# One 64-column product per head and chunk in an RWKV-7 recurrence, with the value map and the state map stacked

## The chip, the cores and the metric

The kernel runs on one core of a Trainium2 chip. TensorE (PE) multiplies, and its weight loads are listed apart as PEld; VectorE (DVE), ScalarE (ACT) and GpSimd (POOL) do elementwise work, and SyncE (SP) issues the DMAs, in order. The metric is the device time of the whole program in microseconds. The kernel before takes 2608.76 us, the median of 3 runs (2606.76 to 2610.3).

## The reference

A hybrid decoder block: RMSNorm, one input projection whose columns go to two token mixers side by side (an S5 state-space mixer and RWKV-7 time mixing), one output projection with a residual, then a squared-ReLU MLP. 2048 tokens, model width 1024, float32. The change lies in the RWKV-7 recurrence: 8 heads of 64, a 64x64 state per head, decayed and updated once per token.

```python
def step(state, inp):
    r_t, d_t, k_t, v_t, kk_t, a_t = inp
    sa = jnp.einsum('bhvk,bhk->bhv', state, -kk_t)
    state = (state * d_t[:, :, None, :]
             + sa[..., None] * (kk_t * a_t)[:, :, None, :]
             + v_t[..., None] * k_t[:, :, None, :])
    return state, jnp.einsum('bhvk,bhk->bhv', state, r_t)
...
_, ys = lax.scan(step, s0, xs)
```

## The kernel before

The program goes through input stages, the recurrence (`rwkv_phase`), the output projection and the MLP; a planner overlaps neighbouring stages. The recurrence takes 64 tokens at a time: 32 chunks, four to a block of 256 tokens, 8 blocks. The 8 heads stand in 4 pairs (`NP`), so that a pair fills 128 partitions: rows 0–63 are its first head, 64–127 its second.

For a chunk, the output and the next state are linear in the chunk's values and in the state before it. `solve` builds the two maps, `chain` applies them:

- `values` (one unit per pair and block) loads k and v of a pair into one zero-padded tile `bk` (each head on its own diagonal block), and q into `qi`. It forms `ps_k` (L853), masks it into `kT` (DVE L857, ACT L858), and transposes v on PE (`ps_v`, L851) into `vT` (ACT L855). Once per block, q is also loaded as `qS` (L840).
- `units` does the same for the other operands: `ps_b` (L817) into `bQ`, `ps_a` (L826) into `aR`. Each unit's last loads and the strips `abd` (L832) feed `invert`.
- `invert` solves the triangular 16-step systems of a block on DVE (`prod`, `Z`, L876/877), with DMAs in and out (`M`, `zd`, `dtc`, `lo`); `join` finishes the inverse with 32x32 products (`ps_x` L898, `ps_u` L905).
- `solve` (per chunk): POOL spreads the inverse (`DT`, L913), PE multiplies (`ps_pq`, L920), ACT copies into a block-diagonal tile `pq` in two halves (L923, L924), and PE forms `ps_f` (L928) and `ps_h` (L930), four 128x128 products each. DVE adds q and the identity to `ps_f`, which gives `gf`, the map from the state (L934, L935), and `kT` to `ps_h`, which gives `hj`, the map from the values (L936).
- `chain` (per chunk, in two halves of two pairs): per pair `ps_s` = `hj`·`vT` (L949) plus `gf`·`S` (L951), both 128 columns, accumulated in one PSUM bank. Rows 64–127 are the next state, scaled by `em` on DVE into the block-diagonal `S` (L957), rows 0–63 the output, copied by ACT (L958) and stored (L963).

The order on PE is written by hand: the loop over chunks n takes, in turn, the first half of `chain`, a pending `ps_v`, the second half, `ps_pq` of chunk n+2, `ps_b` of a unit 13 ahead, `ps_k` of a value unit 5 ahead, `ps_f` and `ps_h` of chunk n+2, and `ps_a`. Units end at chunk 19 and value units at chunk 27. The other engines and SP are ordered by the scheduler. Value loads wait until the tile they overwrite is free: `bk` and `qi` exist twice (`NB`). Every fp32 matmul runs as two passes on PE, each with its own weight load.

Of the kernel before, what the change touches and what calls it, by code (L numbers as in the profile page):

```python
# [15 lines left out]
P = 128  # L16
# [740 lines left out]
def rwkv_phase(K, f_dram, e_dram, n_dram, y_dram, ntok=2048):  # L757
# [7 lines left out]
    with ExitStack() as st:  # L765
# [11 lines left out]
        S = None  # L777
# [20 lines left out]
        mask = lambda t, n: bc(t.rearrange("p (o x) -> p o x", o=1), [P, n, t.shape[1]])  # L798
# [35 lines left out]
        def values(b, B, p):  # L834

            if p == 0:
                kv = kvs[b % 2]
                for n, shape in (("kT", [P, NCH, NP, P]), ("vT", [P, NCH, NP, P]), ("qS", [P, NP, TB])):
                    B[n] = kv.tile(shape, F32, tag=n, name=n)
                nc.sync.dma_start(out=B["qS"], in_=f_dram[:, :, b, RW["q"]].rearrange("t p n -> p t n"))  # L840
            kT, vT = B["kT"], B["vT"]
            i = (b * NP + p) % NB
            bk, qi = bks[i], qis[i]
            load_pair(bk, b, p, RW["k"])
            nc.sync.dma_start(out=qi[:, 0].rearrange("p c x -> p (c x)"), in_=f_dram[p, :, b, RW["q"]])
            for n in range(2):
                ps = pk("ps_" + "kv"[n])
                for u in range(NCH):
                    o = ps[:, u * P:(u + 1) * P]
                    if n:  # L850
                        pe.transpose(out=o, in_=bk[:, n, u], identity=K.ident)  # L851
                    else:
                        pe.matmul(o, bk[:, n, u], qi[:, :, u], start=True, stop=True)  # L853
                if n:
                    act.copy(out=vT[:, :, p], in_=r4(ps))  # L855
                else:
                    B["last"] = v.tensor_tensor(out=kT[:, :, p, 0:64], in0=r4(ps)[:, :, 0:64], in1=mask(c["mk"], NCH), op=ALU.mult)  # L857
                    act.copy(out=kT[:, :, p, 64:128], in_=r4(ps)[:, :, 64:128])  # L858
                    yield
# [48 lines left out]
        def solve(B, u):  # L908

            aR, kT, bQ, qS, dtc, cpl = B["aR"], B["kT"], B["bQ"], B["qS"], B["dtc"], B["cpl"]  # L910
# [10 lines left out]
            pq = pqs[u % 2]  # L921
            psr = ps.rearrange("p (a q x) -> p a q x", a=NP, q=2)
            act.copy(out=pq[0:64, :, :, 0:64], in_=psr[0:64])  # L923
            act.copy(out=pq[64:128, :, :, 64:128], in_=psr[64:128])  # L924
            yield
            psf, psh = pb("ps_f"), pb("ps_h")
            for p in range(NP):
                pe.matmul(psf[:, p * P:(p + 1) * P], pq[:, p, 1], bQ[:, u, p, 64:192], start=True, stop=True)  # L928
            for p in range(NP):
                pe.matmul(psh[:, p * P:(p + 1) * P], pq[:, p, 0], bQ[:, u, p, 64:192], start=True, stop=True)  # L930
            gf = bt.tile([P, NP, 2, 64], F32, tag="gf", bufs=3, name="gf")
            hj = bt.tile([P, NP, P], F32, tag="hj", bufs=3, name="hj")
            pf = psf.rearrange("p (a q x) -> p a q x", a=NP, q=2)
            v.tensor_tensor(out=gf[:, :, 0], in0=pf[:, :, 0], in1=qS[:, :, u * 64:(u + 1) * 64], op=ALU.add)  # L934
            v.tensor_tensor(out=gf[:, :, 1], in0=pf[:, :, 1], in1=bc(ist, [P, NP, 64]), op=ALU.add)  # L935
            B["last"] = v.tensor_tensor(out=f2(hj), in0=psh, in1=f2(kT[:, u]), op=ALU.add)  # L936
            yield gf, hj

        def chain(b, B, u, gf, hj):
            nonlocal S  # L940
            vT = B["vT"]
            yS = Ys[u % 2 * 64:u % 2 * 64 + 64]
            new = Ss[u % 2]

            for p0 in range(0, NP, 2):
                pss = pc("ps_s")
                for p in range(p0, p0 + 2):
                    o = slice((p - p0) * P, (p - p0 + 1) * P)
                    pe.matmul(pss[:, o], hj[:, p], vT[:, u, p], start=True, stop=S is None)  # L949
                    if S is not None:  # L950
                        pe.matmul(pss[:, o], gf[:, p].rearrange("p q x -> p (q x)"), S[:, p], start=False, stop=True)  # L951

                pv = pss[:, 0:2 * P].rearrange("p (a h x) -> p a h x", a=2, h=2)
                for h in range(2):
                    hs = slice(h * 64, h * 64 + 64)
                    e = em[64:128, p0:p0 + 2, h, b * NCH + u:b * NCH + u + 1]
                    v.tensor_tensor(out=new[hs, p0:p0 + 2, hs], in0=pv[64:128, :, h], in1=bc(e, [64, 2, 64]), op=ALU.mult)  # L957
# [3 lines left out]
            S = new  # L961
# [18 lines left out]
        bks, qis = [T([P, 2, NCH, P], f"bk{i}", vp) for i in range(NB)], [T([P, 2, NCH, 64], f"qi{i}", vp) for i in range(NB)]  # L980
# [4 lines left out]
        pqs = [bt.tile([P, NP, 2, P], F32, tag=f"pq{i}", bufs=1, name=f"pq{i}") for i in range(2)]  # L985
        Ss = [bt.tile([P, NP, P], F32, tag=f"S{i}", bufs=1, name=f"S{i}") for i in range(2)]
        Ys = bt.tile([P, 512], F32, tag="Y", bufs=1, name="Y")
        for t in pqs + Ss:
            g.memset(t, 0.0)
# [4 lines left out]
        for h in range(2):  # L994
            nc.sync.dma_start(out=em[64:128, :, h], in_=e_dram[:, h * 64:h * 64 + 64].rearrange("t p n -> p t n"))
# [743 lines left out]
```

## Time and profile before

| | |
|---|---|
| time, median of 3 runs | 2608.76 us |
| the profiled execution | 2615.8 us, its span 2614.0 us, granted clock 0.974 |
| PE, PEld, DVE, ACT, POOL busy | 2447.6, 2026.7, 1844.5, 1301.2, 851.4 us |
| recurrence, first and last `ps_s` | 694.2 and 981.8 us |
| PE busy in 700–740, 900–940 us | 38.49, 34.53 of 40 us |
| share of 16 DMA engines in 700–740 | 0.71 |

Times are microseconds unless marked ns. In a timeline row stand the start, the length, the engine, the line and the instruction, what is written and read, shapes and count, then in brackets the idle time of the engine before it and what ended that. A row of a group has count, busy time and mean ns of one, and idle time before. `L949` is line 949 of the kernel. Matmuls are pipelined, so one lasts longer than the distance to the next; the cost of a series is read from start to start.

### The profile page before, as it was taken

How to read it: one execution, taken by the hardware profiler on the slowest of the kernel's cores; microseconds unless marked ns; L12 is line 12 of the kernel's file. 1: busy time of each engine (PE TensorE's matmuls, PEld its weight loads, DVE VectorE, ACT ScalarE, POOL GpSimd, SP SyncE). 2: the span in 40 equal slices, each digit the busy share in tenths (PEclk: the TensorE clock that was granted, in tenths of full speed). 3: DMA queues.
4: the chain of work that ended last, by engine and by line, in shares of the span. 5: the costliest groups of instructions: out<-in, count | busy, mean ns of one | idle time of the engine just before them, and what ended most of it. 6: DMA issues, size and time to landing. Idle time of an engine off the chain costs nothing.

```text
span 2614.0 us, 38287 instructions
## 1 busy us (share of the span) xinstructions
PE 2447.6 (94%) x13084; PEld 2026.7 (78%) x13084; DVE 1844.5 (71%) x3194; ACT 1301.2 (50%) x2551; POOL 851.4 (33%) x784
## 2 busy tenths in 40 slices
PE   7999988998889888999899999999969999999997
PEld 7887656786889887888688888888857877777775
DVE  7568897479678768666867669776665556655665
ACT  6355536455444446454566667666543323333333
POOL 1058798601222224121123221332102223322323
PEclk9999989999899998999999999999999999999998
DMA  9656748897776644443475666655585545444544
GB/s 290 210 162 177 215 125 235 245 247 186 176 165 154 136 140 163 143 148 127 170 268 204 212 212 212 229 206 202 188 318 177 178 157 169 166 157 154 184 153 161
DMA packets 542131, 491.50 MB, mean 188 GB/s; under 512 B 187280, under 2 KB 444304, under 8 KB 541936
## 3 DMA queue, kind: packets, MB, share of 16 engines
q1 hardware_dynamic: 541648, 488.00, 60.0%
q8 instruction: 104, 1.70, 0.3%
q10 hardware_dynamic: 288, 1.05, 0.1%
q14 instruction: 91, 0.75, 0.1%
HBM read 303.23 MB, written 180.49 MB: 185 GB/s over the span
## 4 chain that ended last, share of the span: by engine, by line
PE 65%; DVE 13%; DMA 12%; issue 3%; ACT 3%; POOL 2%; SPq 2%; POOLq 0%; DVEq 0%; ACTq 0%
PE ps_ua L1328 13%; PE ps_da L1328 9%; PE ps_ux L1328 7%; PE ps_dx L1328 4%; PE ps_ub L1328 3%; PE ps_db L1328 2%; DMA wraw<-in_w_down 2%; PE ps_o L433 2%; PE ps_o L434 2%; PE ps_o L435 2%; PE ps_z L433 1%; PE ps_z L434 1%; PE ps_z L435 1%; DMA wr<-in_w_in 1%; DVE wl L609 1%
## 5 line engine op out<-in xcount | busy, mean ns | idle before, releaser
L1618 POOL TENSOR_TENSOR acc<-acc,c 128x512 f32<-128x512 f32 x128 | 191.1, 1513 | 500.7 <-ACT c L1622 446.6
L1622 ACT COPY c<-ps_da 128x512 f32<-128x512 f32 x192 | 106.3, 588 | 267.9 <-PE ps_da L1328 266.6
L433 PE MATMUL ps_z<-xh,wh 128*128 128x512 f32 x448 | 183.7, 410 | 16.3 <-DVE zr L617 7.5
L1618 DVE TENSOR_TENSOR acc<-acc,ps_dx 128x512 f32<-128x512 f32 x128 | 87.6, 685 | 133.0 <-PE ps_dx L1328 130.3
L435 PE MATMUL ps_z<-xh,wl 128*128 128x512 f32 x448 | 181.2, 405 | 0.0
L434 PE MATMUL ps_z<-xl,wh 128*128 128x512 f32 x448 | 180.8, 404 | 0.0
L374 ACT CAST hh<-hr 128x512 fp32r<-128x512 f32 x96 | 59.6, 621 | 131.7 <-PE ps_da L1328 92.6
L1425 DVE TENSOR_TENSOR wl<-wraw,wh 128x512 fp32r<-128x512 f32 x124 | 103.8, 838 | 29.5 <-ACT wh L1424 29.2
L433 PEld LDWEIGHTS ps_z<-xh,wh 128*128 128x128 f32 x448 | 86.8, 194 | 41.3 <-DVE zr L617 9.3
L609 DVE TENSOR_TENSOR wl<-wr,wh 128x1024 fp32r<-128x1024 f32 x56 | 86.7, 1548 | 36.8 <-ACT wh L608 35.0
L913 POOL TENSOR_TENSOR DT<-dtc,cst 128x128 f32<-128x128 f32 x128 | 56.0, 468 | 156.9 <-PE ps_pq L920 105.4
L1291 POOL TENSOR_TENSOR ws<-wraw 128x512 f32<-128x512 f32 x28 | 41.2, 1471 | 202.1 <-DMA hs_d<-hh 72.8
L433 PE MATMUL ps_o<-woh,ys 128*128 128x512 f32 x256 | 103.3, 404 | 2.5 <-DVE xrow L1225 2.5
L1424 ACT CAST wh<-wraw 128x512 fp32r<-128x512 f32 x124 | 76.1, 616 | 54.0 <-PE ps_ua L1328 34.9
L434 PE MATMUL ps_o<-wol,ys 128*128 128x512 f32 x256 | 102.5, 401 | 0.2 <-DVE wol L1125 0.2
L435 PEld LDWEIGHTS ps_z<-xh,wl 128*128 128x128 f32 x448 | 86.9, 194 | 19.0 <-issue 0.2
L434 PEld LDWEIGHTS ps_z<-xl,wh 128*128 128x128 f32 x448 | 86.8, 194 | 18.6 <-issue 0.9
L435 PE MATMUL ps_o<-woh,ys 128*128 128x512 f32 x256 | 101.2, 399 | 0.0
L1300 POOL TENSOR_TENSOR ws<-wraw,ws 128x512 f32<-128x512 f32 x28 | 41.7, 1488 | 176.9 <-DVE wl L1425 173.6
L1425 DVE TENSOR_TENSOR wl<-ws,wh 128x512 fp32r<-128x512 f32 x93 | 66.8, 721 | 29.5 <-ACT wh L1424 25.0
L1474 DVE TENSOR_TENSOR hh<-hs,hh 128x512 fp32r<-128x512 f32 x96 | 79.7, 830 | 10.5 <-ACT hh L1473 9.7
L1473 ACT CAST hh<-hs 128x512 fp32r<-128x512 f32 x96 | 59.6, 621 | 53.9 <-DVE hs L1490 21.0
(690 smaller groups left out, 8216.6 us busy)
## 6 DMA issues: line engine op xcount, KB each, us to landing
hs_d<-hh SPq DMA_DIRECT2D x256, 256.0 KB
hs<-hs_d SPq DMA_DIRECT2D x128, 512.0 KB
wraw<-in_w_up SPq DMA_DIRECT2D x62, 512.0 KB
wr<-in_w_in SPq DMA_DIRECT2D x56, 512.0 KB
hr_d<-c SPq DMA_DIRECT2D x96, 256.0 KB
hr<-hr_d SPq DMA_DIRECT2D x96, 256.0 KB
xrow<-in_x SPq DMA_DIRECT2D x32, 512.0 KB
wraw<-in_w_down SPq DMA_DIRECT2D x16, 1024.0 KB
```

Of the source, the lines that this page charges most:

```text
L374: nc.scalar.copy(out=hi, in_=raw)
L433: K.nc.tensor.matmul(out, lh, rh, start=i == 0, stop=False)
L434: K.nc.tensor.matmul(out, lh, rl, start=False, stop=False)
L435: K.nc.tensor.matmul(out, ll, rh, start=False, stop=i == n - 1)
L609: v.tensor_tensor(out=wl, in0=wr, in1=wh.bitcast(F32), op=ALU.subtract)
L1328: K.nc.tensor.matmul(ps, a[k], b[k], start=start and k + i == 0, stop=k == n - 1 and i == 2, skip_group_check=True)
L1424: act.copy(out=hi, in_=o)
L1425: v.tensor_tensor(out=lo, in0=o, in1=hi.bitcast(F32), op=ALU.subtract)
L1473: act.copy(out=hi, in_=o)
L1474: v.tensor_tensor(out=lo, in0=o, in1=hi.bitcast(F32), op=ALU.subtract)
L1618: add = lambda eng, o, s: eng.tensor_tensor(out=o, in0=o, in1=s, op=ALU.add)
L1622: act.copy(out=t, in_=ps)
```

## The change

The two maps of one head are put on top of each other in one 128x128 tile `gh`: rows 0–63 act on the chunk's values, rows 64–127 on the state. The operand is stacked in the same way: `SV` holds, per chunk, the transposed values in rows 0–63 and the state in rows 64–127. So `chain` runs one product of 64 columns per head and chunk, where a pair had two of 128 columns. To get there:

- `KQ` takes the place of `kT`, `qS` and the identity: per head, masked `ps_k` above, q and the identity below. q is loaded into it by two DMAs per value unit; the identity is copied once, by 16 DVE instructions at the recurrence's start.
- v gets a dense tile `vc` of its own, and `bk` holds k alone.
- `pq` is no longer block-diagonal: one ACT copy of 128 partitions. `ps_f` and `ps_h` become one `ps_h`, eight products with 64 rows each, by turns from the first head's rows and the second's, into two banks; two DVE additions of `KQ` give `gh`.
- the state is written into the next chunk's place in `SV`, two DVE instructions per chunk in place of four. The clearing of `pq` and `S` on POOL goes; half of `SV`'s first chunk is cleared.

PE's instructions over one chunk, before (`pq0`, `aq1` and so on are buffers of the tiles above):

```order
L817 MATMUL ps_b_8356<-aq1_5202,ba1_5200 128x192 x2
L853 MATMUL ps_k_8366<-qi1_6803,bk1_6801 128x128 x4
L928 MATMUL ps_f_8373<-bQ_6910,pq0_6811 128x128 x4
L930 MATMUL ps_h_8374<-bQ_6910,pq0_6811 128x128 x4
L826 MATMUL ps_a_8388<-aq1_5202,ba1_5200 128x128 x4
L949 MATMUL ps_s_8400<-vT_7680,hj_8223 128x128
L951 MATMUL ps_s_8400<-S0_6813,gf_8222 128x128
...
L851 MATMUL ps_v_8408<-cst_60,bk1_6801 128x128 x4
L949 MATMUL ps_s_8414<-vT_7680,hj_8223 128x128
L951 MATMUL ps_s_8414<-S0_6813,gf_8222 128x128
...
L920 MATMUL ps_pq_8430<-aR_6909,DT_8423 128x128 x4
```

and with the change:

```order
L816 MATMUL ps_b_9424<-aq1_5202,ba1_5200 128x192 x2
L848 MATMUL ps_k_9437<-qi1_6826,bk1_6822 128x128 x4
L927 MATMUL ps_h_9446<-bQ_7649,pq_9411 128x128
L927 MATMUL ps_h_9447<-bQ_7649,pq_9411 128x128
...
L825 MATMUL ps_a_9459<-aq1_5202,ba1_5200 128x128 x4
L943 MATMUL ps_s_9471<-SV0_6802,gh_9294 128x64 x4
L856 MATMUL ps_v_9478<-cst_60,vc1_6824 64x128 x4
L943 MATMUL ps_s_9484<-SV0_6802,gh_9294 128x64 x4
L918 MATMUL ps_pq_9499<-aR_7648,DT_9492 128x128 x4
```

The order of the steps stays. The two rows of `ps_h` stand for four such pairs in a row, and each row of `ps_s` now covers half a chunk (before, the two rows L949 and L951 stood twice per half).

DVE's queue at the recurrence's start (`L617`, `L377` and `L715` are the last of the input stage, `up` opens the first `join`; `Z` and `prod` are the inversion of the second block). Before, this stretch holds no copy but the two of `qi`; with the change:

```order
L974 COPY KQ1_6801<-cst_60 64x4x64 x4
L617 SCALAR_TENSOR_TENSOR zv_6722<-ps_z_6693,omu_1853,sh_6718 128x512
...
L377 TENSOR_TENSOR sql_6766<-zr_6687,sqh_6765 128x512
...
L715 TENSOR_TENSOR zr_6687<-ps_bv_6764,zv_6722 128x512
L886 STREAM_TRANSPOSE up_6846<-dtc_5394 128x512
...
L974 COPY KQ0_6800<-cst_60 64x4x64 x5
L979 COPY qi0_6825<-cst_60 128x256
```

Eight copies into `KQ1` stand ahead of `zv` and `sql`, eight into `KQ0` between `up` and `qi`.

SP's queue of loads about a block's boundary, before:

```order
L832 DMA abd_7615<-bQ_7614 32x16x32 x4
L804 DMA ba1_5200<-f_d_68 64x8x64 x2
L880 DMA zd_7138<-Z_7718 64x16x32 x2
L865 DMA M_8234<-abd_7615 64x32x32 x2
...
L882 DMA dtc_7787<-zd_7138 128x1x512
L813 DMA aq1_5202<-f_d_68 128x256
L804 DMA bk1_6801<-f_d_68 64x8x64 x2
L891 DMA lo_8396<-zd_7138 32x512 x2
```

and with the change:

```order
L843 DMA KQ0_6800<-f_d_68 64x4x64
L842 DMA bk1_6822<-f_d_68 64x4x64
L831 DMA abd_7166<-bQ_7165 32x16x32 x4
L803 DMA ba1_5200<-f_d_68 64x8x64 x2
L863 DMA M_7747<-abd_7166 64x32x32 x2
L878 DMA zd_6927<-Z_7237 64x16x32 x2
...
L812 DMA aq1_5202<-f_d_68 128x256
L842 DMA bk1_6822<-f_d_68 64x4x64
L844 DMA qi1_6826<-f_d_68 128x256
L845 DMA vc1_6824<-f_d_68 128x256
...
L880 DMA dtc_7306<-zd_6927 128x1x512
L889 DMA lo_7910<-zd_6927 32x512 x2
```

The loads of the value units stand ahead of `dtc` now, and those into `KQ` in a bunch before the strips `abd`.

The diff, without unchanged neighbours:

```diff
-        S = None
...
-        mask = lambda t, n: bc(t.rearrange("p (o x) -> p o x", o=1), [P, n, t.shape[1]])
+        mask = lambda t, n, rows=P: bc(t.rearrange("p (o x) -> p o x", o=1), [rows, n, t.shape[1]])
...
         def values(b, B, p):
-            if p == 0:
-                kv = kvs[b % 2]
-                for n, shape in (("kT", [P, NCH, NP, P]), ("vT", [P, NCH, NP, P]), ("qS", [P, NP, TB])):
-                    B[n] = kv.tile(shape, F32, tag=n, name=n)
-                nc.sync.dma_start(out=B["qS"], in_=f_dram[:, :, b, RW["q"]].rearrange("t p n -> p t n"))
-            kT, vT = B["kT"], B["vT"]
+            KQ, SV = KQs[b % 2], SVs[b % 2]
+            B["KQ"], B["SV"] = KQ, SV
             i = (b * NP + p) % NB
-            bk, qi = bks[i], qis[i]
-            load_pair(bk, b, p, RW["k"])
+            bk, vc, qi = bks[i], vcs[i], qis[i]
+            for h in range(2):
+                hp = slice(h * 64, h * 64 + 64)
+                nc.sync.dma_start(out=bk[hp, :, hp], in_=f_dram[p, hp, b, RW["k"]].rearrange("p (c x) -> p c x", x=64))
+                nc.sync.dma_start(out=KQ[64:128, :, h, p, 0:64], in_=f_dram[p, hp, b, RW["q"]].rearrange("p (c x) -> p c x", x=64))
             nc.sync.dma_start(out=qi[:, 0].rearrange("p c x -> p (c x)"), in_=f_dram[p, :, b, RW["q"]])
-            for n in range(2):
-                ps = pk("ps_" + "kv"[n])
-                for u in range(NCH):
-                    o = ps[:, u * P:(u + 1) * P]
-                    if n:
-                        pe.transpose(out=o, in_=bk[:, n, u], identity=K.ident)
-                    else:
-                        pe.matmul(o, bk[:, n, u], qi[:, :, u], start=True, stop=True)
-                if n:
-                    act.copy(out=vT[:, :, p], in_=r4(ps))
-                else:
-                    B["last"] = v.tensor_tensor(out=kT[:, :, p, 0:64], in0=r4(ps)[:, :, 0:64], in1=mask(c["mk"], NCH), op=ALU.mult)
-                    act.copy(out=kT[:, :, p, 64:128], in_=r4(ps)[:, :, 64:128])
-                    yield
+            nc.sync.dma_start(out=vc.rearrange("p c x -> p (c x)"), in_=f_dram[p, :, b, RW["v"]])
+            ps = pk("ps_k")
+            for u in range(NCH):
+                pe.matmul(ps[:, u * P:(u + 1) * P], bk[:, u], qi[:, :, u], start=True, stop=True)
+            for h in range(2):
+                hp = slice(h * 64, h * 64 + 64)
+                B["last"] = v.tensor_tensor(out=KQ[0:64, :, h, p, 0:64], in0=r4(ps)[hp, :, 0:64], in1=mask(c["mk"][hp], NCH, 64), op=ALU.mult)
+                act.copy(out=KQ[0:64, :, h, p, 64:128], in_=r4(ps)[hp, :, 64:128])
+            yield
+            ps = pk("ps_v")
+            for u in range(NCH):
+                pe.transpose(out=ps[0:64, u * P:(u + 1) * P], in_=vc[:, u], identity=K.ident)
+            act.copy(out=SV[0:64, :, p], in_=r4(ps)[0:64])
...
-            aR, kT, bQ, qS, dtc, cpl = B["aR"], B["kT"], B["bQ"], B["qS"], B["dtc"], B["cpl"]
+            aR, bQ, dtc, cpl = B["aR"], B["bQ"], B["dtc"], B["cpl"]
...
                 pe.matmul(ps[:, p * P:(p + 1) * P], m2(DT, p), aR[:, u, p], start=True, stop=True)
-            pq = pqs[u % 2]
-            psr = ps.rearrange("p (a q x) -> p a q x", a=NP, q=2)
-            act.copy(out=pq[0:64, :, :, 0:64], in_=psr[0:64])
-            act.copy(out=pq[64:128, :, :, 64:128], in_=psr[64:128])
+            pq = bt.tile([P, NP, P], F32, tag="pq", name="pq")
+            act.copy(out=f2(pq), in_=ps)
             yield
-            psf, psh = pb("ps_f"), pb("ps_h")
+            ph = [pb("ps_h") for _ in range(2)]
             for p in range(NP):
-                pe.matmul(psf[:, p * P:(p + 1) * P], pq[:, p, 1], bQ[:, u, p, 64:192], start=True, stop=True)
-            for p in range(NP):
-                pe.matmul(psh[:, p * P:(p + 1) * P], pq[:, p, 0], bQ[:, u, p, 64:192], start=True, stop=True)
-            gf = bt.tile([P, NP, 2, 64], F32, tag="gf", bufs=3, name="gf")
-            hj = bt.tile([P, NP, P], F32, tag="hj", bufs=3, name="hj")
-            pf = psf.rearrange("p (a q x) -> p a q x", a=NP, q=2)
-            v.tensor_tensor(out=gf[:, :, 0], in0=pf[:, :, 0], in1=qS[:, :, u * 64:(u + 1) * 64], op=ALU.add)
-            v.tensor_tensor(out=gf[:, :, 1], in0=pf[:, :, 1], in1=bc(ist, [P, NP, 64]), op=ALU.add)
-            B["last"] = v.tensor_tensor(out=f2(hj), in0=psh, in1=f2(kT[:, u]), op=ALU.add)
-            yield gf, hj
-        def chain(b, B, u, gf, hj):
-            nonlocal S
-            vT = B["vT"]
+                for h in range(2):
+                    hs = slice(h * 64, h * 64 + 64)
+                    pe.matmul(ph[h][:, p * P:(p + 1) * P], pq[hs, p], bQ[hs, u, p, 64:192], start=True, stop=True)
+            gh = bt.tile([P, 2, NP, P], F32, tag="gh", bufs=3, name="gh")
+            for h in range(2):
+                B["last"] = v.tensor_tensor(out=f2(gh[:, h]), in0=ph[h], in1=f2(B["KQ"][:, u, h]), op=ALU.add)
+            yield gh,
+        def chain(b, B, u, gh):
+            SV = B["SV"]
+            n = b * NCH + u
             yS = Ys[u % 2 * 64:u % 2 * 64 + 64]
-            new = Ss[u % 2]
             for p0 in range(0, NP, 2):
                 pss = pc("ps_s")
                 for p in range(p0, p0 + 2):
-                    o = slice((p - p0) * P, (p - p0 + 1) * P)
-                    pe.matmul(pss[:, o], hj[:, p], vT[:, u, p], start=True, stop=S is None)
-                    if S is not None:
-                        pe.matmul(pss[:, o], gf[:, p].rearrange("p q x -> p (q x)"), S[:, p], start=False, stop=True)
-                pv = pss[:, 0:2 * P].rearrange("p (a h x) -> p a h x", a=2, h=2)
-                for h in range(2):
-                    hs = slice(h * 64, h * 64 + 64)
-                    e = em[64:128, p0:p0 + 2, h, b * NCH + u:b * NCH + u + 1]
-                    v.tensor_tensor(out=new[hs, p0:p0 + 2, hs], in0=pv[64:128, :, h], in1=bc(e, [64, 2, 64]), op=ALU.mult)
+                    for h in range(2):
+                        o = (2 * (p - p0) + h) * 64
+                        pe.matmul(pss[:, o:o + 64], gh[:, h, p], SV[:, u, p, h * 64:h * 64 + 64], start=True, stop=True)
+                if n + 1 < nb * NCH:
+                    to = SVs[(n + 1) // NCH % 2][64:128, (n + 1) % NCH, p0:p0 + 2].rearrange("p a (h x) -> p (a h) x", h=2)
+                    v.tensor_tensor(out=to, in0=pss[64:128, 0:2 * P].rearrange("p (a x) -> p a x", a=4),
+                                    in1=bc(em[64:128, 2 * p0:2 * p0 + 4, n:n + 1], [64, 4, 64]), op=ALU.mult)
                 act.copy(out=yS[:, p0 * P:(p0 + 2) * P], in_=pss[0:64, 0:2 * P])
                 if p0 == 0:
                     yield
-            S = new
...
         vp = pool(name="rwv", bufs=1)
-        bks, qis = [T([P, 2, NCH, P], f"bk{i}", vp) for i in range(NB)], [T([P, 2, NCH, 64], f"qi{i}", vp) for i in range(NB)]
+        KQs, SVs = ([T([P, NCH, *d], f"{n}{i}", kvs[i]) for i in range(2)] for n, d in (("KQ", [2, NP, P]), ("SV", [NP, P])))
+        for t in KQs:
+            for h in range(2):
+                for u in range(NCH):
+                    v.tensor_copy(t[64:128, u, h, :, 64:128], bc(ist[64:128], [64, NP, 64]))
+        g.memset(SVs[0][64:128, 0], 0.0)
+        bks, vcs, qis = ([T([P, *d], f"{n}{i}", vp) for i in range(NB)] for n, d in (("bk", [NCH, P]), ("vc", [NCH, 64]), ("qi", [2, NCH, 64])))
         for i in range(NB):
             g.memset(bks[i], 0.0)
             v.tensor_copy(qis[i][:, 1], bc(ist, [P, NCH, 64]))
         bt = pool(name="rwbt", bufs=2, side="right")
-        pqs = [bt.tile([P, NP, 2, P], F32, tag=f"pq{i}", bufs=1, name=f"pq{i}") for i in range(2)]
-        Ss = [bt.tile([P, NP, P], F32, tag=f"S{i}", bufs=1, name=f"S{i}") for i in range(2)]
         Ys = bt.tile([P, 512], F32, tag="Y", bufs=1, name="Y")
-        for t in pqs + Ss:
-            g.memset(t, 0.0)
         psum = {n: pool(name="rwps" + n, bufs=k, space=PSUM) for n, k in (("b", 2), ("c", 2))}
         pb, pc = (lambda name, q=psum[n]: q.tile([P, 512], F32, tag="ps", name=name) for n in "bc")
-        em = bt.tile([P, NP, 2, ntok // 64], F32, tag="em", bufs=1, name="em")
+        em = bt.tile([P, 2 * NP, ntok // 64], F32, tag="em", bufs=1, name="em")
         for h in range(2):
-            nc.sync.dma_start(out=em[64:128, :, h], in_=e_dram[:, h * 64:h * 64 + 64].rearrange("t p n -> p t n"))
+            nc.sync.dma_start(out=em[64:128, h::2], in_=e_dram[:, h * 64:h * 64 + 64].rearrange("t p n -> p t n"))
...
```

## The prediction

> **What bounds the kernel now.** I read the windows of busy time first, to find the recurrence and what is short in it, then the groups of instructions by line, then the timeline of the matmuls, and the waits last. A window row gives start and end, the length, then busy us and the number of instructions of PE, PEld, DVE, ACT and POOL, the granted clock, the share of the DMA engines and GB/s:
>
> ```profile
> 640.00:665.00 25.00, 18.09 (x167) 14.35 (x167) 23.16 (x60) 9.78 (x21) 12.43 (x20) 0.73 0.52 155
> 700.00:740.00 40.00, 38.49 (x412) 37.53 (x413) 35.38 (x129) 20.58 (x53) 8.46 (x23) 1.00 0.71 161
> 900.00:940.00 40.00, 34.53 (x389) 33.29 (x388) 31.79 (x104) 16.02 (x34) 9.76 (x24) 1.00 0.49 116
> 940.00:985.00 45.00, 40.15 (x427) 37.99 (x426) 27.59 (x65) 25.53 (x50) 11.52 (x27) 1.00 0.57 170
> 985.00:1030.00 45.00, 37.55 (x203) 31.51 (x203) 40.28 (x78) 31.16 (x66) 22.83 (x13) 0.85 0.58 193
> ```
>
> Up to 665 us VectorE (DVE) is full. From 700 to 985 TensorE (PE) is, with DVE 4 to 18 us behind it in each window. The recurrence's 32 chunks run there, so work taken from PE counts in full only up to DVE's distance. After 985 DVE leads again, in the output projection, which the change does not edit.
>
> One chunk without the inverse's products, PE alone (start, length, line, product, passes):
>
> ```profile
> 763.93 0.49 PE L949 MATMUL ps_s<-vT,hj 128*128 128x128 f32 x2
> 766.26 1.06 PE L920 MATMUL ps_pq<-aR,DT 128*128 128x128 f32 x8
> 767.15 1.47 PE L817 MATMUL ps_b<-aq,ba 128*128 128x192 f32 x8
> 768.45 1.05 PE L853 MATMUL ps_k<-qi,bk 128*128 128x128 f32 x8
> 769.34 1.06 PE L928 MATMUL ps_f<-bQ,pq 128*128 128x128 f32 x8
> 770.24 1.06 PE L930 MATMUL ps_h<-bQ,pq 128*128 128x128 f32 x8
> 772.02 0.39 PE L949 MATMUL ps_s<-vT,hj 128*128 128x128 f32 x2
> ```
>
> A chunk is 772.02 − 763.93 = 8.09 us with no gap. Each fp32 matmul is two passes, x8 is four matmuls. Eight passes of 128 columns take 769.34 − 768.45 = 0.89 us, 111 ns each; eight of 192 take 768.45 − 767.15 = 1.30 us, 163 ns each. The four pairs of ps_s matmuls are 16 passes, 1.78 us a chunk; ps_f and ps_h together are 16 too, again 1.78.
>
> **The narrower products.** The change runs eight ps_s matmuls of 64 columns where eight of 128 stood: the same 16 passes and 16 weight loads of 128x128, half the columns. What such a pass costs hangs on whether columns or the weight load sets the 111 ns. From 128 to 192 columns a pass grew by 52 ns, 0.81 ns a column; by that line a pass of 64 would be 59 ns. But the trace has short passes with full-width weights:
>
> ```profile
> 29.45 0.29 PEld L131 LDWEIGHTS ps_lam<-cst,lam 32*128 32x128 f32 x2
> 29.46 0.40 PE L131 MATMUL ps_lam<-cst,lam 32*128 32x32 f32 x2
> L131 PEld LDWEIGHTS ps_lam<-cst,lam x4: 181/182/184, 29.5 to 31.3; 32*128 32x128 f32 x4
> L131 PE MATMUL ps_lam<-cst,lam x4: 271/282/292, 29.5 to 31.3; 32*128 32x32 f32 x4
> ```
>
> Two loads of 128 columns end after 0.29 us and one lasts 0.182, so the second starts 0.108 behind the first, though only 32 columns stream; the two matmuls start 0.40 − 0.282 = 0.12 us apart. So I price a 64-column pass at 108 to 120 ns, against 111: between −0.05 and +0.14 us a chunk. I take 0. The low bound is the column line, 16 × (59 − 111) ns = −0.83 us.
>
> The Trainium skill ("TensorE: Matmul & The Clock Gate", section "LDWEIGHTS (loading the stationary operand)") says that a weight load takes as many ns as it has columns, divided by 1.2, whatever its rows: 107 here. The 108 ns agrees, and by it ps_s stays at 1.7 us. Its section "Back-to-back issue gap" lets an isolated matmul of up to 64 columns go in about 60 cycles; that would be the column line's outcome, weighed as a rival below.
>
> **ps_f and ps_h become one ps_h by heads.** Eight matmuls of 128 rows become eight of 64 rows, alternating between rows 0–63 and 64–127, into two banks. If the halves run one after the other nothing is gained: 1.78 us stays. If side by side, 8 × 111 ns = 0.89 us. The trace shows two row groups at work where one head's products meet the next's (32-row tiles):
>
> ```profile
> 655.39 3.24 PE L898 MATMUL ps_x<-up,bQ 32*32 32x32 f32 x61 [1.49 <-DVE up L888]
> 658.41 0.26 PE L905 MATMUL ps_u<-lo,up 32*32 32x32 f32 x1
> 658.45 0.24 PE L898 MATMUL ps_x<-up,bQ 32*32 32x32 f32 x1
> 658.48 0.24 PE L905 MATMUL ps_u<-lo,up 32*32 32x32 f32 x1
> 658.51 0.24 PE L898 MATMUL ps_x<-up,bQ 32*32 32x32 f32 x1
> ```
>
> Inside the first row 61 passes start over 658.41 − 655.39 = 3.02 us, 50 ns apart. Where ps_u of the first head starts while ps_x of the second still has passes, the two lines alternate every 0.03 us: each stream keeps nearly its own pace. So I take 0.89, −0.89 us a chunk.
>
> The Trainium skill ("TensorEngine Tiling (Array Packing)", section "Key Properties") says tiles load and multiply in parallel, and that changing the tiling mode drains TensorE. The second half speaks against this change, and the trace prices it:
>
> ```profile
> 162.95 0.48 PE L669 MATMUL ps_w<-stk,low0h 128*128 128x512 f32 x1
> 163.36 0.50 PE L670 MATMUL ps_w<-stk,lowl 64*128 64x512 f32 x1
> 163.79 0.50 PE L433 MATMUL ps_z<-xh,wh 128*128 128x512 f32 x1
> 164.13 0.39 PE L434 MATMUL ps_z<-xl,wh 128*128 128x512 f32 x1
> 164.35 0.39 PE L435 MATMUL ps_z<-xh,wl 128*128 128x512 f32 x1
> 788.80 1.06 PE L920 MATMUL ps_pq<-aR,DT 128*128 128x128 f32 x8
> 789.79 2.11 PE L898 MATMUL ps_x<-up,bQ 32*32 32x32 f32 x64
> ```
>
> Into 64 rows the step is 0.41 us, out of it 0.43, the next 0.34, where 0.22 is the pace: 0.19 + 0.21 + 0.12 = 0.52 at most. Into ps_x it is 789.79 − 788.80 − 0.89 = 0.10 us alone. A chunk has one more such round trip, ps_k to ps_h to ps_a; between 0.3 and 0.52 I take 0.41. So PE has −0.89 + 0.41 = −0.48 us a chunk.
>
> **DVE and ACT.** These groups change (line, shapes, count, busy us, mean ns, idle before); under them one row of the waits of 892 to 942, and two of the chain of waits:
>
> ```profile
> L957 DVE TENSOR_TENSOR S<-ps_s,em 64x128 f32<-64x128 f32 x127 | 37.3, 294 | 11.7 <-PE ps_s L951 9.0
> L936 DVE TENSOR_TENSOR hj<-ps_h,kT 128x512 f32<-128x512 f32 x32 | 22.0, 687 | 2.0 <-PE ps_h L930 0.7
> L924 ACT COPY pq<-ps_pq 64x512 f32<-64x512 f32 x32 | 18.6, 580 | 0.8
> L934 DVE TENSOR_TENSOR gf<-ps_f,qS 128x256 f32<-128x256 f32 x32 | 13.5, 421 | 9.7 <-PE ps_f L928 9.5
> PE ps_f L928 <- ACT pq L924: 4.6, 5, 1.4
> 932.76 2.89 DMA zd<-Z
> 942.75 2.11 PE ps_x L898 x64
> ```
>
> Free size sets these: 687 ns for 512, 421 for 256. DVE before: 3 × 421 (two gf, one kT) + 687 + 4 × 294 = 3.13 us a chunk; after: 2 × 687 (gh) + 2 × 421 (state) + 2 × 421 (KQ) = 3.06. Nothing. ACT loses the second pq copy, 0.58 us, and gains a second KQ copy off the path. The pq copy is on the path where PE waits for it: in 892 to 942, where the seven chunks 20–26 have no unit ps_b or ps_a, five waits give back at most 5 × 0.58 = 2.9 us. There PE would gain 7 × 0.48 + 2.9 = 6.3 us, but the chain of waits runs there through the last block's inversion on DVE: zd is written at 932.76, and ps_x starts at 942.75, just when PE is free. DVE's part does not get shorter. Between 0 and −6.3 I take −3.
>
> Every ps_s product now waits for the state, not half of them; but the state was needed before too by the second matmul (L951, 0.22 us behind the first), and no L951 waits in the trace: 0. In the last five chunks ps_pq follows ps_h and needs the bank that gh empties, 0.69 us, against the 0.48 gained: 0.
>
> **Setup.** Sixteen DVE copies of the identity are added. Eight stand ahead of the last zv and sql, which the first ps_x waits for through ps_bv, zr and up, on a DVE full to 23.2 of 25 us:
>
> ```profile
> 653.11 0.79 PE L675 MATMUL ps_bv<-sql,ones2r 128*128 128x512 f32 x1 [0.22 <-DVE sql L377]
> 656.90 1.01 DVE L983 COPY qi<-cst 128x256 f32<-128x256 f32 x2
> 669.68 5.70 DMA ba<-f_d
> ```
>
> A copy of that length is 0.54 us beside POOL's clears (L983); by the 256-wide adds it is 0.42 otherwise, so 8 of them are 3.4 us. The other eight fall ahead of the first bQ, 3.4 more, but the wait for ba, 5.70 us from 669.68, covers them. I take +3; without that cover 7, and 0 if the 1.84 us of slack and PE's gaps take it.
>
> **Loads.** A value unit has 6 DMAs on SP where 3.25 stood, in packets of much the same size:
>
> ```profile
> L804 SPq DMA_DIRECT2D bk<-f_d x64: 573/595/1257, 661.3 to 941.5; - x64
> 781.45 2.04 PE L853 MATMUL ps_k<-qi,bk 128*128 128x128 f32 x8 [4.84 <-DMA lo<-zd]
> ```
>
> 2.75 × 0.6 = 1.6 us more of SP a chunk, in 8.1 at least. At a block's boundary PE stands 4.84 us until loads land that queue on SP behind the inverse's. What stands behind the new loads comes up to 1.6 us later; against that, k's load no longer waits for ps_v, its neighbour in the old tile, and stands ahead of dtc at a boundary. I take 0, between −11 and +11 (seven boundaries by 1.6 either way).
>
> **Sum.** Chunks 0–19: 20 × −0.48 = −9.6; 20–26: −3; the last five 0; setup +3; loads 0: −9.6 us. The profiled run is 2615.8 us (span 2614.0 and 1.8 around it), so 2606.2 on its scale; it lies 7.0 above the median of 2608.76, so **2599**. With setup, the stretch 892 to 942 and the drain at their bounds it is 2590 to 2608.
>
> **Rivals.** (a) Columns set the pass. Then PE loses 0.83 more a chunk, 27 us over 32, of which DVE's 3.1 us of distance in the window 700:740 hold back about 3 in its five chunks: 24, so 2575. For it: the line from 128 to 192; against it: the 108 ns loads. 0.12. (b) The halves do not overlap, each drain is paid: +0.41 × 32 = 13.1, setup +3, the copy −2: +14, 2623. It decides once the eight ps_h matmuls take more than 1.78 − 0.41 = 1.37 us. For it: no row shows 64-row tiles, 128 wide, side by side; against it: the alternating rows. 0.13. (c) The loads or DVE give the gain back: boundaries +11, or inversion and setup at their bounds: 2605 to 2615, no change that shows. For it: PE already stands there for DMA. 0.25.
>
> **How the numbers follow.** Forecast 0.50, (a) 0.12, (b) 0.13, (c) 0.25. Some 0.2% (5 us) is what a measurement of this kernel tells from no change. Faster: 0.46 of the forecast, (a), a little of (c): 0.63. Same: the rest of the forecast, half of (c): 0.17. Slower: (b) and the rest of (c): 0.20. The range reaches from (a) to (b): 2573 to 2621.
>
> **What will show it.** ps_s: 16 passes still near 1.75 us; 0.95 means (a). ps_h: 0.9 us for its 16 passes, the two banks in turn; 1.78 means (b). The step from ps_h to ps_a and the first ps_a: 0.4 us above pace together. First ps_x three us later than 655.4. The gap ahead of ps_k at boundaries near 5 us; 6.5 means (c). I am wrong in kind if the steady chunk (8.09 us) does not come to about 7.6.

## The result

The changed kernel takes 2628.87 us, the median of 6 runs (2621.57 to 2636.74), against 2608.01 before on the same chip (2606.3 to 2612.68): ratio 1.007, interval 1.0054 to 1.0085. In a later measurement of the same two kernels it was 1.0041 (1.0026 to 1.0056). So it is slower by 0.4 to 0.7%, where 0.4% faster was forecast, and outside the range. The profiled execution is the quickest of its six, 2621.57 us with a span of 2619.8; the one of the kernel before was 7 us above its median. The two traces can therefore show where time went, but not all of the difference of the medians.

The windows of busy time of the changed kernel, columns as before (busy us of PE, PEld, DVE, ACT and POOL, then the granted clock):

```profile
640.00:665.00 25.00, 14.39 (x158) 11.40 (x156) 24.21 (x58) 8.27 (x17) 9.85 (x15) 0.70 0.38 111
700.00:740.00 40.00, 38.55 (x419) 36.59 (x419) 34.25 (x109) 18.49 (x48) 9.10 (x24) 0.96 0.74 170
900.00:940.00 40.00, 35.81 (x388) 33.62 (x388) 31.11 (x90) 14.61 (x35) 9.46 (x25) 0.87 0.47 106
940.00:985.00 45.00, 34.10 (x362) 32.31 (x363) 18.09 (x36) 17.18 (x36) 8.92 (x24) 0.81 0.41 107
985.00:1030.00 45.00, 36.64 (x219) 31.95 (x218) 39.81 (x76) 29.72 (x61) 22.04 (x13) 0.78 0.61 209
```

The granted clock stands out: 0.96, 0.87, 0.81 and 0.78 where it was 1.00, 1.00, 1.00 and 0.85. Summed from the clock's record, TensorE ran at half speed for 55 us between 690 and 985, against 14 before.

A chunk of the changed kernel, PE alone:

```profile
773.51 1.05 PE L848 MATMUL ps_k<-qi,bk 128*128 128x128 f32 x8
775.01 1.16 PE L927 MATMUL ps_h<-bQ,pq 64*128 64x128 f32 x16 [0.45 <-ACT pq L920]
776.11 1.16 PE L825 MATMUL ps_a<-aq,ba 128*128 128x128 f32 x8
777.10 1.00 PE L943 MATMUL ps_s<-SV,gh 128*128 128x64 f32 x8
777.94 0.60 PE L856 MATMUL ps_v<-cst,vc 128*64 128x128 f32 x4
778.38 1.00 PE L943 MATMUL ps_s<-SV,gh 128*128 128x64 f32 x8
779.22 1.11 PE L918 MATMUL ps_pq<-aR,DT 128*128 128x128 f32 x8
```

Here the working held. Eight narrow passes take 777.94 − 777.10 = 0.84 us, 105 ns each on the mean. The second starts 59 ns after the first, which is the column line's figure; all that follow start 111 ns apart, like passes of 128 columns. So half the columns gain nothing while each pass brings its own load of 128. The 16 passes of ps_h take 776.11 − 775.01 = 1.10 us with the drain into them, ps_a 0.99 in place of 0.89: side by side, two switches of together some 0.3 us. Chunks of that kind that wait for nothing take 7.5 us (3, 15, 18), where they took 8.1.

So the time went elsewhere. Four stretches, from the starts of the last ps_z, of the first and last ps_s, of the last block's `M` load and of its first ps_x:

| us | before | after | |
|---|---|---|---|
| last ps_z to first ps_s (setup) | 48.4 | 54.5 | +6.1 |
| first ps_s to the last `M` (chunks 0–19) | 203.4 | 198.4 | −5.0 |
| last `M` to the last block's ps_x | 45.1 | 52.5 | +7.4 |
| that ps_x to the last ps_s | 39.1 | 43.7 | +4.6 |

The sum is +13.1 us, of the 20.9 by which the medians differ; the second execution of the changed kernel gives +14.8. Cut at the first ps_s of a chunk, chunks 0–19 take 201.5 us in place of 204.9, chunks 20–26 take 67.5 in place of 58.4, and the last five 25.5 in place of 24.3. So the loss of the table's last two rows lies almost whole in chunks 20–26. From the last ps_s to the first product of the MLP both need 274.5 to 274.8 us, so nothing comes back. What follows ran 7 us shorter in this execution of the changed kernel (1350.7 against 1357.7 us); over all the executions here it lies between 1344.7 and 1358.0, whatever the edit.

**Setup.** The first ps_x came later as forecast. What was not: a new wait inside the start. One row each from the timeline, the waits of 655 to 700 and the groups of 655 to 1000:

```profile
656.32 0.79 PE L675 MATMUL ps_bv<-sql,ones2r 128*128 128x512 f32 x1 [3.12 <-DVE sql L377]
PE ps_v L856 <- ACT KQ L852: 3.2, 3, 1.4
L856 PE MATMUL ps_v<-cst,vc 128*64 128x128 f32 x128 | 20.5, 284 | 4.1 <-ACT KQ L852 4.0
```

ps_bv comes 3.2 us later than the 653.11 of before; counted from the last ps_z, it and the first ps_x come 3.9 us later. Behind the first ps_x the start takes another 2.3 us more. There ps_v, which shares one PSUM bank with ps_k, waits until that bank is read out, and this is now four instructions in two engines, where two did it. These 3.2 us of waits cost less than that, since PE's wait ahead of ps_b falls from 4.2 to 2.5 us. The 6.1 us of the table is on the high side: four further executions with this setup take 54.2 to 56.3 us, and two of the kernel before with other edits 50.3 and 50.4 in place of 48.4.

**The last block.** The inversion on DVE from its first to its last instruction, and then the stretch from the last first ps_x to the last ps_s, before (two rows) and after (two, with PE's wait for the inverse and two rows of PE's timeline under them):

```profile
902.20:932.00 29.80, 24.82 (x304) 23.76 (x303) 27.48 (x92) 12.79 (x27) 9.76 (x24) 1.00 0.46 113
942.70:981.80 39.10, 34.70 (x381) 32.94 (x382) 23.57 (x56) 21.93 (x44) 10.72 (x25) 1.00 0.56 169
```

```profile
903.70:940.60 36.90, 32.41 (x354) 30.34 (x355) 29.92 (x89) 13.71 (x31) 9.40 (x24) 0.86 0.38 98
950.60:994.30 43.70, 38.94 (x392) 37.01 (x392) 21.77 (x40) 19.69 (x39) 10.84 (x25) 0.80 0.47 139
PE ps_x L896 <- DVE up L886: 7.5, 2, 5.7
912.80 3.26 PE L896 MATMUL ps_x<-up,bQ 32*32 32x32 f32 x64 [1.83 <-DVE up L886]
915.99 2.08 PE L848 MATMUL ps_k<-qi,bk 128*128 128x128 f32 x8
```

DVE is idle for 7.0 of the 36.9 us, against 2.3, and has 2.4 us more of chunk work in between; the inversion's own instructions take the same time (17.3 and 17.5 us). Of DVE's waits there, 2.5 us are for PE and 3.3 for DMAs. The third row is a wait of 898 to 995 that before did not have: PE stands until the last two blocks' inverses are there. The last two rows are the first of these waits and what follows it. The clock halves at 913.1 us, and ps_k and ps_h take twice their time while DVE is in the middle of the last block's inversion.

### The profile page after: what moved, and what is told of

Its sections match the earlier page's. It is cut to its first block, busy times and chain, and to the rows that moved or that the text cites. A ratio compares the mean times of both kernels' runs of the same rounds, so it can differ in the third digit from the quotient of the medians.

```text
span 2619.8 us, 38382 instructions
## 1 busy us (share of the span) xinstructions
PE 2451.8 (94%) x13092; PEld 2021.2 (77%) x13092; DVE 1853.7 (71%) x3144; ACT 1290.5 (49%) x2551; POOL 851.3 (32%) x781
## 4 chain that ended last, share of the span: by engine, by line
PE 64%; DVE 15%; DMA 9%; issue 4%; ACT 4%; POOL 2%; SPq 2%; POOLq 0%; DVEq 0%; ACTq 0%
PE ps_ua L1320 13%; PE ps_da L1320 10%; PE ps_ux L1320 7%; PE ps_dx L1320 5%; PE ps_ub L1320 3%; PE ps_db L1320 3%; DMA wraw<-in_w_down 2%; PE ps_o L435 2%; PE ps_o L433 2%; PE ps_o L434 2%; DMA dtc<-zd 1%; PE ps_z L433 1%; PE ps_z L434 1%; PE ps_z L435 1%; PE ps_b L816 1%
## 5 line engine op out<-in xcount | busy, mean ns | idle before, releaser
L1417 DVE TENSOR_TENSOR wl<-ws,wh 128x512 fp32r<-128x512 f32 x93 | 65.8, 710 | 26.0 <-ACT wh L1416 17.5
```

Of the source, the lines that this page charges most:

```text
L1417: v.tensor_tensor(out=lo, in0=o, in1=hi.bitcast(F32), op=ALU.subtract)
```

## Why the clock halves

In this stretch of the changed kernel PE is never idle, and yet the clock drops at 721.9 us, just ahead of the second ps_s:

```profile
718.57 2.11 PE L903 MATMUL ps_u<-lo,up 32*32 32x32 f32 x64
720.61 1.10 PE L943 MATMUL ps_s<-SV,gh 128*128 128x64 f32 x8
721.55 0.69 PE L856 MATMUL ps_v<-cst,vc 128*64 128x128 f32 x4
722.03 1.81 PE L943 MATMUL ps_s<-SV,gh 128*128 128x64 f32 x8
723.63 1.93 PE L918 MATMUL ps_pq<-aR,DT 128*128 128x128 f32 x8
725.40 1.47 PE L816 MATMUL ps_b<-aq,ba 128*128 128x192 f32 x8
718.50:721.90 3.40, 3.40 (x78) 3.29 (x77) 3.27 (x10) 1.61 (x5) 0.52 (x2) 1.00 0.56 163
```

The record changes only at marks 3.41 us apart, so I counted what streamed in each such window: every pass by its columns at 0.83 ns, weighted by the rows in use over 128. The 0.83 comes from passes of 192 columns, which at half clock start 320 ns apart, 1.67 ns a column (64 more columns cost 0.81 a column above). Between 690 and 985 us, over all 14 profiled executions of this study, 96 windows at full clock come to less than 0.375 of their length, and 92 of them are followed by a halved one; 957 come to more, and none is. The bound was chosen on these same windows. Without the weight by rows it fails: then 49 of the halved windows follow one above the bound. The window above has 0.36: ps_u fills 32 of 128 rows, and a narrow ps_s streams for half of its time. Before, the same place had 128 columns in every pass, and only three windows fell below, each with a gap in PE.

The Trainium skill ("TensorE: Matmul & The Clock Gate", section "What's actually happening") puts the return to half rate at one idle window of about 3.4 us or more. The length of the window agrees with the 3.41 us; that it must be idle does not, since the quoted one is full of instructions. On the weight load the page's formula gives an estimate of 107 ns for 128 columns; the passes measured here, 105 ns on the mean and 111 inside a row, agree with it.

## The experiments

Each is compared with runs of the kernel before on its own chip, so only ratios compare across chips. A stretch is read from one execution of each.

**Columns back in the changed kernel.**

```diff
-  pe.matmul(pss[:, o:o + 64], gh[:, h, p], SV[:, u, p, h * 64:h * 64 + 64], ...)
+  pe.matmul(pss[:, o:o + P], gh[:, h, p], SV[:, u, p], ...)   # o in steps of P
```

> The changed kernel with ps_s at 128 columns again: each head's product moves the 64 columns of its own head and of its neighbour, and only its own are read. More work for TensorE, the rest untouched. Theory A (the clock is halved after any 3.41 us window in which the array streams too little, columns weighted by rows, under about 0.38 of the window; the narrow ps_s halves what streams in an unchanged time): half-clock time between 690 and 985 us falls from 58 us to 20 to 35, time 8 to 14 us below the changed kernel's 2628.9. Theory B (the loss is the setup and the loads on SP, the clock only follows waits for DMA): eight half ps_s passes cost 0.84 us now and 0.89 wide, so 3 us slower than the changed kernel, the same half-clock time.

Ratio 1.0068 (1.0049 to 1.0087): no faster. The windows below 0.375 fall from 11 to 6, but the half-clock time only from 55 to 48 us. 31 us of it lie in chunks 20–26, where PE waits 8.4 us for `up` in place of 7.5; the last stretch took 51.9 us at a clock of 0.77. Theory A, by which the narrow columns alone cost it, fell; the 3 us of theory B lie within the interval.

**Columns halved in the kernel before.**

```diff
-  pe.matmul(pss[:, o], hj[:, p], vT[:, u, p], ...)
+  pe.matmul(pss[:, o][:, 0:64], hj[:, p], vT[:, u, p, 0:64], ...)   # and gf with S likewise
```

> The kernel before with one thing narrowed: every ps_s product moves 64 columns in place of 128, with the same weight loads and the same number of passes. The second head's columns are left out, and the first head's are read twice in their place; nothing else differs. Theory A: a pass still takes 105 to 111 ns (weight load), so PE gains 0 to 0.1 us a chunk, but half-clock windows appear at the joins; 5 to 15 us slower than before. Theory B: no more half-clock time than before (14 us between 690 and 985), time within 4 us of before. If columns set the pass after all: 0.8 us a chunk less, some 20 us faster.

Ratio 1.0013 (1.0000 to 1.0026), half-clock time 34 us in place of 14, the last inversion 32.2 in place of 29.8. Most chunks without a join stay at 8.0 to 8.3 us: halving the columns frees nothing, and it costs some 3 us, at most 7. Theory A was right on the clock here, theory B on the time. The windows below 0.375 rise from 3 to 6.

**Identity copies on ScalarE.**

```diff
-  v.tensor_copy(t[64:128, u, h, :, 64:128], ...)
+  act.copy(out=t[64:128, u, h, :, 64:128], ...)
```

> The changed kernel with the sixteen copies of the identity on ScalarE in place of VectorE. Theory B for its setup part: the first ps_x comes 3 us sooner (655.5 in place of 658.6) and the first ps_s 3 to 5 us sooner, time 3 to 5 us below the changed kernel. Theory A says nothing on the setup, and expects the half-clock time after 690 us unchanged at about 58 us.

Ratio 1.0010 (0.9992 to 1.0028). First ps_s 51.3 us after the last ps_z, 3.2 sooner; the half-clock time stays at 51. The first ps_x, expected 3 us sooner, is only 0.5 sooner against the last ps_z (12.9 us, in place of 13.4, and 9.5 before): on ScalarE the copies hold up the same start (with them later, in the last version below, it is 10.1). The rest is gained behind it, though ps_v still waits 3.2 us. The gain is more than the setup's: the last inversion takes 33.7 us, the last stretch 40.1 and chunk 25 only 9.9 in place of 18.2, without any edit there. Where drops fall moved with the start, so part of it may be their place; that part is not settled.

**ps_h by heads, not by turns.**

```diff
-  for p in range(NP):
-      for h in range(2):
+  for h in range(2):
+      for p in range(NP):
```

> The changed kernel with the eight ps_h products by heads, four of the first head's rows and then four of the second's, in place of by turns. If the turns are what lets the two halves run side by side: ps_h takes 1.6 to 1.8 us with its drain in place of 1.09, chunks are 0.5 to 0.7 us longer, time 5 to 15 us above the changed kernel's. If the halves run side by side in any order: 1.1 us and no change in time.

The rows of ps_h there and of the products around it:

```profile
766.70 1.05 PE L848 MATMUL ps_k<-qi,bk 128*128 128x128 f32 x8
767.68 1.71 PE L927 MATMUL ps_h<-bQ,pq 64*128 64x128 f32 x16
769.32 1.16 PE L825 MATMUL ps_a<-aq,ba 128*128 128x128 f32 x8
```

1.64 us in place of 1.10, so it is the turns that put the halves side by side. The ratio, 1.0066 (1.0044 to 1.0088), lies on the changed kernel's first and above its second, and the 5 to 15 us expected do not show; 0.55 us more a chunk did not lengthen chunks 0–19 (195.1 us, at a clock of 0.99 and without the waits for qi, against 198.4 at 0.93).

**More matmuls ahead of the last two joins.**

```diff
   ps = pp("ps_x")
+  if h == 0 and B["b"] >= 6:
+      for i in range(16):
+          pe.matmul(ps[:, i % 4 * P:i % 4 * P + P], K.ident, K.ident, start=True, stop=True)
```

> The changed kernel with 16 more matmuls of 128x128 (32 passes, 3.6 us), whose result is overwritten, ahead of the first ps_x of the last two joins, where TensorE stands waiting for dtc. Theory A' (those waits halve the clock, and the half clock then delays what DVE's queue waits for): half-clock time between 905 and 985 us falls from 31 us to under 15, the last block's inversion on DVE shortens from 36.9 to 30 to 33 us, chunk 25 from 18.2 to 12 to 14, time 4 to 8 us below the changed kernel's. Theory C (DVE's chain from the strips abd through inversion, zd and dtc to ps_x sets the last joins by itself): inversion and chunk 25 stay within 2 us, time unchanged.

```profile
905.90:938.90 33.00, 28.49 (x345) 26.94 (x346) 27.35 (x83) 11.19 (x26) 8.79 (x23) 0.95 0.40 95
951.80:990.50 38.70, 32.83 (x393) 31.29 (x392) 21.41 (x40) 19.33 (x39) 8.73 (x20) 0.96 0.58 160
```

Ratio 1.0022 (1.0004 to 1.0039). The two windows answer to those of the last block: 33.0 in place of 36.9 us, 38.7 in place of 43.7, at clocks of 0.95 and 0.96; chunk 25 is 13.1 us in place of 18.2. The fill delays ps_x itself: it starts 12.9 us after the inversion's end, in place of 10.0. So the two stretches are 8.9 us shorter, but from the last `M` to the last ps_s it is 89.9 us in place of 96.2, 6.3 less, and chunks 20–26 take 61.6 in place of 67.5. The half-clock time in 905 to 985 falls from 28 to 7 us. On the whole time the interval overlaps that of the changed kernel's 1.0041. The same lines in the kernel before:

> The kernel before with the same 16 matmuls ahead of ps_x in the last two joins. There the clock is full from 870 to 985 us and TensorE waits little. Theory A' (in the changed kernel they pay by keeping the clock full): nothing to gain here, 0 to 5 us slower than before, last inversion 29 to 31 us. If they pay in another way, by shifting what DVE and TensorE wait for: faster here too, by 3 us or more.

Ratio 1.0004 (0.9992 to 1.0017), inversion 28.3 us, clock 1.00: nothing to gain there, as theory A' had it. In its trace chunks 20–26 take 64.8 us in place of 58.4. The same fill costs 6.4 us where PE does not wait, and saves 5.9 where PE's waits halve the clock.

**Units two chunks further ahead**, in the changed kernel and in the one before.

```diff
-AHEAD = 13
+AHEAD = 15          # and units 13 and 14 run before the first chunk
```

> The changed kernel with the loading units two chunks further ahead (15 in place of 13; units 13 and 14 run before the first chunk, so it starts some 5 us later), and so each block's inversion begins two chunks sooner. Theory C: the last join no longer waits, chunk 25 takes 7 to 10 us in place of 18.2, chunk 21 7 to 10 in place of 14.5; time 4 to 12 us below the changed kernel's. Theory B (setup and loads): chunk 25 follows only in part, the later start eats it, time within 4 us of the changed kernel's.

> The kernel before with the units 15 ahead, as the same edit on the other side. Theory C: there the last inversion and TensorE meet (ps_x at 942.7 with TensorE free at 942.5), so the edit brings little: chunk 25 from 10.4 to 7 to 9, later start of 5 us against it, time within 4 us of before.

After: 1.0059 (1.0039 to 1.0079). Chunk 25 falls to 9.5 us and chunk 21 to 10.3, much as theory C said, and the last inversion to 31.6; but the first ps_s comes 12.1 us later, the clock was 0.89 over chunks 0–19, and the time did not fall as theory C expected. Before: 0.9979 (0.9960 to 0.9999), its chunk 25 at 10.2: the gain came in chunks 8, 12 and 16, whose waits at the block boundaries go (8.2 to 8.7 us in place of 13.0 to 14.8), which I had not expected. Side by side, with the same edit in both, chunks 20–26 take 50.8 us after and 55.2 before, and PE waits for no inverse there: without that wait the change gains 4.4 us in these chunks, about the 3 of the forecast.

**q copied by GpSimd.**

```diff
-  nc.sync.dma_start(out=KQ[64:128, :, h, p, 0:64], in_=f_dram[p, hp, b, RW["q"]]...)
+  g.tensor_copy(KQ[64:128, :, h, p, 0:64], qi[h * 64:h * 64 + 64, 0])
```

> The changed kernel with q copied into KQ by GpSimd from the tile that ps_k uses, in place of two DMAs per value unit, so four DMAs a unit. Theory B (SP's longer queue holds back dtc and the block's loads): the gap from zd's last issue to dtc's falls from 5.3 us to 4, ps_x of joins 6 and 7 comes 1 to 3 us sooner, time 3 to 6 us below the changed kernel's. Theory C: no change beyond 2 us, or slower where GpSimd's copies delay DVE.

The waits of PE for loads in chunks 0–19, first of the changed kernel, then of this one:

```profile
PE ps_k L848 <- DMA qi<-f_d: 6.8, 3, 3.2
```

```profile
PE ps_k L849 <- DMA qi<-f_d: 1.3, 1, 1.3
```

Ratio 1.0023 (1.0005 to 1.0041). The wait for qi, which stands behind the longer queue on SP, nearly goes, the last `M` comes 194.4 us after the first ps_s, 4 sooner, and the ps_x of block 6's join 3.1 sooner against the last ps_z. The last join is no sooner, since that inversion took 39.7 us at a clock of 0.70. The gap from zd's last issue to dtc's, ahead of block 6's join, did not fall as expected (5.5 us, in place of 5.3). Without q's DMAs these chunks take 3 to 4 us less than in the two executions of the changed kernel; but the run with ps_h by heads has all six DMAs and took 195.1, so the loads' share is not settled.

**The changed kernel again, and the edits together**, on one chip. In the last, the copies for the second `KQ` also stand behind the first chunks' pq copies, and GpSimd copies q.

> The changed kernel itself, on the chip of the other runs of this call: 0.5 to 0.85% slower than before, half-clock time between 690 and 985 us near 55 us, the last block's inversion 35 to 40 us long.

> The changed kernel with both: identity copies on ScalarE and the 16 more matmuls ahead of ps_x in the last two joins. If setup and the half clock of the last joins are the two losses, and add: first ps_s 51 us after the last ps_z (54.5 in the changed kernel), the last inversion 32 us, last ps_x to last ps_s 39 us, the last ps_s 338 to 341 us after the last ps_z (349.0 and before 336.0); time 10 to 16 us below the changed kernel's, 0 to 0.2% above before. If the two are one effect seen twice: no better than either alone, 0.1 to 0.25% above before.

> As the run with both, and the identity copies of the second KQ tile only after the first chunks' pq copies, and q copied into KQ by GpSimd. By the same sum: first ps_s 49 to 50 us after the last ps_z, M of the last block 195 us later, last ps_s 332 to 337 after the last ps_z; time at or up to 0.3% below before's. If GpSimd's copies slow DVE: no better than the run with both.

Ratios: 1.0041 (1.0026 to 1.0056), 1.0005 (0.9989 to 1.0020), 0.9979 (0.9962 to 0.9997). The first is the changed kernel's second execution: 42 us of half clock, not the 55 expected, with a last inversion of 38.3 us. So the half-clock time as a sum does not set the loss; what lies in chunks 20–26 (27 us here, 24 in the first) does more. Setup and fill together are 10 us below the changed kernel, but not clearly below the copies on ScalarE alone (1.0010); the last ps_s came 346.6 us after the last ps_z, where 338 to 341 were expected, so that the two add is not shown. With the other two edits it is 2611.41 us against 2615.51 before. Its three stretches, the first ps_s to the last `M`, the last inversion, the last ps_x to the last ps_s:

```profile
693.80:885.70 191.90, 180.37 (x1966) 169.11 (x1965) 170.29 (x535) 89.12 (x233) 64.05 (x166) 0.96 0.68 151
891.20:920.70 29.50, 25.41 (x301) 23.65 (x299) 25.05 (x78) 8.81 (x20) 9.34 (x24) 0.88 0.30 78
938.10:978.30 40.20, 35.33 (x392) 33.57 (x392) 22.02 (x41) 20.56 (x42) 8.15 (x18) 0.87 0.56 163
```

Chunks 0–19 take 11.5 us less than before the change (10.3, cut at chunk 20's first ps_s), about the forecast gain. The last inversion is as short as before though the clock is 0.88, with fewer instructions of DVE in the stretch (78 against 92): so the clock is not its only cause. How much the order on DVE adds stays open. Chunks 20–26 take 63.4 us here, the fill with them, 5.0 more than before the change.

## Why the prediction was wrong, by its steps

- **Narrow products: right.** 105 ns a pass on the mean, 0 us gained, and halving the columns in the kernel before gave 1.0013. Rival (a) fell.
- **ps_h: right.** 1.10 us with its drain, 1.64 without the turns. The step out of 64 rows and into them was sized at 0.41 us and came to 0.31. Rival (b) gave nearly the right time (2623) for a wrong reason: the halves do overlap. The ends of the range, 2573 and 2621, lie 2 us below the times of (a) and (b) that they are said to be.
- **Setup: mis-sized.** +3 forecast, +6.1 measured in these two traces, some 5 over all of them. 3.9 us stand ahead of the first ps_x, where 3.4 were worked out. The other 2.3 lie behind it, where nothing was forecast: a second KQ copy on ACT, "off the path", holds the bank that ps_v needs, and PE waits 3.2 us for it. How much of the 2.3 is that and how much the other eight copies stays open.
- **Chunks 0–19: right per chunk, half lost between them.** −9.6 forecast, −5.0 measured. With q's loads off SP it was −9.0, and −11.5 in the last version. In this kernel the clock was 0.93 against 0.97 before; in its second execution it was 0.97 and the stretch took 197.5 us, −5.9. What took the rest there the runs do not tell.
- **Loads: "I take 0" held against the kernel before.** PE's waits for loads in these chunks, `lo`, `qi` and `aq`, are 7.4 us (9.4 in the second execution) against 10.0 before, and the longest ahead of ps_k is 3.2, where 5 was forecast. The 3 to 4 us that came with q off SP, as far as they are the loads', are a gain that the change left lying.
- **Chunks 20–26: the step that failed.** "Between 0 and −6.3 I take −3" came to +9.1. I had seen that the last inversion meets PE at 942.5, and had bounded the loss at nothing: if DVE does not get shorter, the time stays. But the inversion itself became longer, 36.9 us in place of 29.8. DVE's queue holds the inversion and the chunks in turns. PE, ahead of DVE now, waits 7.5 us for the two last inverses, its clock halves (24 us of half clock in these chunks, none before), and the chunk work that DVE takes in between stretches. Three things speak for this chain: the fill took 5.9 of the 9.1 us away though it costs 6.4 us where no clock is lost; with the units further ahead the wait is gone and the change gains 4.4; and over ten executions of the changed kernel and its variants these chunks take 50.8 to 63.4 us where the clock was halved for up to 10 us in them, and 67.5 to 75.7 where for 24 or more. How much the order on DVE adds is open.
- **The last five chunks: "0" came to +1.2.**
- **Rival (c)** named the right places (inversion and setup) but priced them as the loss of the gain alone: it ended at no change, and the case of both going past it was left out of the range.
- **Clock:** the working took the granted clock as given. Nothing in it asked what the change does to it, though the profile before holds three drops in chunks 0–19, each behind a gap in PE.

## What to carry to other kernels

Shorter matmuls of the same count save nothing while each brings a full-width weight load, and they lower what the array streams: count columns times rows per 3.4 us window before and after, and where a window comes near the 0.375 of full found here, a halved clock belongs in the sum. Where two engines pass work back and forth in a loop with no slack, a gain on one is not bounded by zero: let it run ahead of the other and the wait it meets can cost more than it gained. When one read-out is split by rows into two per engine, look at who needs the bank next.

## What the runs showed that I had not expected

- The granted clock went with the rows and columns streamed, not with whether PE has instructions: 92 of 96 windows below 0.375 were followed by half clock, none of 957 above.
- Sixteen matmuls whose result is thrown away, ahead of each of two joins, shortened chunks 20–26 by 5.9 us (ratio 1.0022, against 1.0041 and 1.0070), and gained nothing (1.0004) where the clock was full.
- The same kernel stood at 1.0070 in one measurement and at 1.0041 in another, with intervals that barely overlap.
